# An attention stage whose engine order becomes one planned list, with the first keys and queries placed ahead of the values

## The chip, the core and the metric

The kernel runs on one core of a Trainium2 chip. A core has a matrix engine (TensorE, PE in the profile; its weight loads are shown as PEld), a vector engine (VectorE, DVE), a scalar engine (ScalarE, ACT), a general engine (GpSimd, POOL) and a sync engine (SyncE, SP) that here only issues transfers. Each engine executes its own instructions in the order in which the program wrote them; an instruction whose operand isn't ready holds up all behind it on that engine. Matrix products go to PSUM, eight banks of 128 x 512 numbers; everything else lies in SBUF.

The metric is the device time of one execution in microseconds (us). Three runs of the kernel before took 1886.28, 1887.10 and 1887.19 us, median 1887.1.

## The reference

Two decoder layers work on 512 tokens of width 1024. Layer 0 mixes tokens with a convolution, layer 1 with stick-breaking attention; each has a feed-forward block before and after. Keys and values come from layer 0's output, queries from layer 1:

```python
u = rms_norm(h, mix_norm[layer])
q = split_heads(u @ attn_w_q[i])
o = stick_breaking_attention(q, k_shared, v_shared)
h = h + o @ attn_w_o[i]
```

For each of 16 heads of width 64 the attention computes, with the strict causal mask:

```python
z = q @ k.T * scale
log_remain = reverse_cumsum(log_sigmoid(-z)) - log_sigmoid(-z)
weights = where(causal, exp(log_sigmoid(z) + log_remain), 0)
o = weights @ v
```

## The kernel before

Everything is in 32-bit floats. For precision a matrix product is made of three: each operand is split into a high part (a rounding copy, on ACT) and a low part (the rest, a subtraction on DVE), and `mm3` multiplies high by high, high by low and low by high. Channels lie on the 128 partitions, so a 512 x 1024 matrix is eight tiles of 128 x 512, `res[0]` to `res[7]` for the residual.

The program is a row of stages: feed-forward 0, convolution, feed-forward 1, feed-forward 2, attention, feed-forward 3. The feed-forward blocks (`planned`) and most of the convolution are written as lists: the code adds steps to a `Plan`, each with its engine, an estimated duration, the tiles it reads and writes, and a rank. `Plan.issue` simulates the engines with these durations. Among the steps that could start it takes the one with the earliest start, and of equal ones the one with the lowest rank, and gives its buffers out. Then it emits the steps in the order found, inside a `manual_schedule` block, which keeps that order on PE, DVE, ACT and POOL. SP isn't among these engines. A step marked `port` (the copies on DVE) and every POOL step exclude each other in the simulation. Outside such a block the framework chooses the order by a simulation of its own. In the kernel before, all of attention is left to the framework.

Attention (lines 1273 to 1473) has these parts:

- The residual is sent away to memory (`away`, L1274), because the heads' outputs `ov` take its place; after the last use of a chunk it is brought back (L1461).
- Constants: triangles, the mask and the two matrices `swap`.
- The norm row `rq` (`n_mix.factor`, L1305): token sums on PE (`ss_mix`), an inverse root in a dozen small DVE operations, a diagonal, two matmuls that spread it, a copy on ACT (L389) and a multiplication by the scale on DVE (L1306).
- `project_values(i)` makes the values of two pairs of heads: two weight units and four blocks of 24 matmuls of 256 columns (`pv`), with a copy on ACT and a subtraction on DVE each.
- `project_keys(p)` makes the keys and queries of one pair: 24 matmuls of 512 columns each (`pk`, `pq`), splits, and transfers between partition halves. The queries are multiplied by `rq` behind the product (L1344).
- `head(p, e)` makes one head in three groups of scores (512, 384 and 512 columns). For a group: the scores `z` on PE; Abs, Exp and Ln on ACT (L1390 to L1392); a combination on DVE (L1393); a split in `sh` and `sl` (L1396, L1397, the 384-column subtraction on POOL); triangle sums on PE back into `z` (L1382); Exp on ACT (L1423, `w`); a split in `wh` and `wl` (L1426, L1427); products with the values into `av` (L1433, L1435). At the end of a head a copy `low` (L1439), a matmul with `swap` and a copy into `ov` (L1441). `sh` and `sl` have one buffer for each group; in the last four heads (`DIRECT`) the sums of later groups read those of the earlier ones.
- The output products: `split` of each chunk of `ov` into `oh` and `ol`, then `output` for eight outputs of eight chunks (`po`). For outputs 2 to 5 (`FIRST`) the product over the first six chunks is made ahead and added to the residual, and the last two chunks follow later. Behind each output stand an addition to the residual (L1467) and the next norm's chunk: a scaled copy, its low part, a square and a sum.

PSUM has four banks for `z`, two for `av`, two for `pj` (shared by `pv`, `pk`, `pq` and `po`). Weights come in units of 128 x 1024: three buffers each for the raw unit, its high and its low part; `unit` hands out the one fetched before and fetches the next, and `weight_order` fixes in which order they come.

The order in which the program writes the projections between the heads is a table; entry p + 1 stands behind the heads of pair p, entry 0 ahead of all heads:

```python
PROJECTIONS = (
    (("v", 0), ("kq", 0)), (("kq", 1), ("kq", 2)), (("v", 1),), (("kq", 3), ("kq", 4)), (("v", 2),),
    (("kq", 5), ("kq", 6)), (("v", 3),), (("kq", 7),),
)
```

Of the kernel before, what the change touches and what calls it, by code (L numbers as in the profile page):

```python
# [14 lines left out]
P = 128  # L15
# [24 lines left out]
for _n, _c in _COLS:  # L40
# [34 lines left out]
    (("v", 0), ("kq", 0)), (("kq", 1), ("kq", 2)), (("v", 1),), (("kq", 3), ("kq", 4)), (("v", 2),),  # L75
# [4 lines left out]
FIRST, SIX = (2, 3, 4, 5), 6  # L80
STS = 1
# [27 lines left out]
class Plan:  # L109
# [8 lines left out]
    def __init__(self, room, lag=None):  # L118
        self.room, self.steps, self.last, self.lag = dict(room), [], {}, lag or {}
        self.held, self.kept = {}, ()  # L120
# [19 lines left out]
    def issue(self):  # L140
# [14 lines left out]
        freeing, uses = [], {}  # L155
# [4 lines left out]
        while ready or freeing:  # L160
            best = None
            for n, t in ready.items():
                engine = steps[n][0]
                t = max(t, free.get(engine, 0.0), now)
                if steps[n][6] and port[1] != engine:
                    t = max(t, port[0])
                new = [x for x in steps[n][5] if first[x] == n and x.slot is None]
                if any(len(room[x.kind]) < sum(y.kind == x.kind for y in new) for x in new):
                    continue
                key = (t, steps[n][4])  # L170
                if best is None or key < best[0]:
                    best = (key, n, new)
# [9 lines left out]
            for x in new:  # L182
                x.slot = room[x.kind].pop(0)
# [23 lines left out]
def decoder_kernel(ctx, tc, xin, gu, dna, dnb, pw1, pw2, kq, wv, wo, out):  # L207
# [53 lines left out]
    def weight_order():  # L261
# [25 lines left out]
        for d in range(NC):  # L287
            yield wo[d][:, SIX * P :] if d in FIRST else wo[d]
# [953 lines left out]
    with ExitStack() as c1:  # L1242
# [30 lines left out]
        for c in range(NC):  # L1273
            nc.sync.dma_start(away[:, c * T : (c + 1) * T], res[c])  # L1274
        ov = res
        with ExitStack() as c:
            ap = pool(c, "at")
            ps = pool(c, "psat", space=PSUM)
            ntri = ap.tile([P, P], F32R, name="ntri")
            none = ap.tile([P, P], F32R, name="none")  # L1280
            tri = ap.tile([P, P], F32, name="tri", tag="a", bufs=3)
            G.affine_select(
                out=tri, in_=ones, compare_op=ALU.is_ge, fill=0.0, base=0,
                pattern=[[-1, P]], channel_multiplier=1,
            )
            V.tensor_scalar_mul(ntri, tri, -1.0)

            identb = ap.tile([P, P], BF16, name="identb")
            V.tensor_copy(identb, ident)
            mask = ap.tile([P, T], BF16, name="mask")  # L1290
            V.memset(mask, 0.0)
            V.tensor_scalar_mul(mask[:, :P], tri, MASKED)
            V.tensor_scalar_mul(mask[:, 256:384], ones, MASKED)
            V.tensor_scalar_mul(mask[:, 384:], tri, MASKED)
            V.tensor_scalar_mul(none, ones, -1.0)

            swap = []
            for e in range(2):
                t = ap.tile([P, P], F32R, name=f"swap{e}")
                G.memset(t.bitcast(F32), 0.0)  # L1300
                V.tensor_copy(t[:, HALVES[e][0]], ident[:, HALVES[e][1]])
                swap.append(t)


            rq = n_mix.factor(ps, ("z", "z"), bufs=Z_BANKS)  # L1305
            V.tensor_scalar_mul(rq, rq, HD ** -0.5)  # L1306
            keys, values = {}, {}

            def project_values(i):
                w = [unit() for h in range(2)]  # L1310
                for p in (2 * i, 2 * i + 1):

                    values[p] = ap.tile([P, 4, 4, HD], F32R, name=f"vs{p}", tag="vs", bufs=4)
                for b in range(4):
                    pv = ps.tile([P, T], F32, name=f"pv{i}_{b}", tag="pj", bufs=PJ_BANKS)
                    for k in range(NC):
                        x = at(kvx[k], b * P, P)
                        m = at(w[k // 4], (k % 4) * 256, 256)
                        mm3(pv[:, :256], x, m, k == 0, k == NC - 1)
                    for q in range(2):  # L1320
                        vs = values[2 * i + q]
                        sl = pv[:, q * P : (q + 1) * P].rearrange("p (e d) -> p e d", e=2)
                        A.copy(vs[:, b, 0::3, :], sl)
                        V.tensor_sub(vs[:, b, 1:3, :], sl, vs[:, b, 0::3, :].bitcast(F32))

            def project_keys(p):
                w = unit()
                pk = ps.tile([P, T], F32, name=f"pk{p}", tag="pj", bufs=PJ_BANKS)
                for k in range(NC):
                    mm3(pk, at(w, k * P, P), kvx[k], k == 0, k == NC - 1)  # L1330


                ks = [ap.tile([P, T], F32R, name=f"ks{p}_{e}", tag=f"ks{e}", bufs=3) for e in range(2)]
                kl = tp.tile([P, T], F32R, name=f"kl{p}", tag="sq", bufs=2)
                for e, (own, other) in enumerate(HALVES):
                    A.copy(ks[e][own, :], pk[own, :])
                    V.tensor_sub(kl[own, :], pk[own, :], ks[e][own, :].bitcast(F32))
                    nc.sync.dma_start(ks[e][other, :].bitcast(F32), kl[own, :].bitcast(F32))
                w = unit()
                pq = ps.tile([P, T], F32, name=f"pq{p}", tag="pj", bufs=PJ_BANKS)  # L1340
                for k in range(NC):
                    mm3(pq, at(w, k * P, P), n_mix.x[k], k == 0, k == NC - 1)
                t = tp.tile([P, T], F32, name=f"qt{p}", tag="sq", bufs=2)
                V.tensor_mul(t, pq, rq)  # L1344
                qs = [ap.tile([P, T], F32R, name=f"qs{p}_{e}", tag=f"qs{e}", bufs=3) for e in range(2)]

                ql = [ap.tile([P, T], F32R, name=f"ql{p}_{e}", tag=f"ql{e}", bufs=2) for e in range(2)]
                for e, (own, other) in enumerate(HALVES):
                    A.copy(qs[e][own, :], t[own, :])
                    nc.sync.dma_start(qs[e][other, :].bitcast(F32), qs[e][own, :].bitcast(F32))  # L1350
                    G.memset(ql[e][other, :].bitcast(F32), 0.0)
                    V.tensor_sub(ql[e][own, :], t[own, :], qs[e][own, :].bitcast(F32))
                keys[p] = (ks, qs, ql)

            def head(p, e):


                vs = values[p]
                ks, qs, ql = keys[p]
                h = 2 * p + e  # L1360
                rows = HALVES[e][0]
                z = []
                for g, blocks in enumerate(GROUPS):
                    zt = ps.tile([P, T], F32, name=f"z{h}_{g}", tag="z", bufs=Z_BANKS)
                    n = sum(T - T0[i] for i in blocks)
                    if g == 0:
                        PE.matmul(zt, identb, mask, start=True, stop=False)
                    o = 0
                    for i in blocks:
                        m, blk = T - T0[i], slice(i * P, (i + 1) * P)  # L1370
                        PE.matmul(zt[:, o : o + m], ks[e][:, blk], qs[e][:, T0[i] :],
                                  start=g > 0, stop=False)
                        PE.matmul(zt[:, o : o + m], ks[e][:, blk], ql[e][:, T0[i] :],
                                  start=False, stop=i == 3)
                        o += m
                    if g > 0:
                        PE.matmul(zt[:, :P], identb, mask[:, :P], start=False, stop=True)
                    z.append(zt[:, :n])

                def add(dst, st, pair, a, b):  # L1380
                    for m in pair:
                        PE.matmul(dst, st, m[:, a:b], start=False, stop=True,  # L1382
                                  skip_group_check=True)

                pav = ps.tile([P, T], F32, name=f"av{h}", tag="av", bufs=AV_BANKS)
                later, behind = None, []
                for g, blocks in enumerate(GROUPS):
                    n = z[g].shape[-1]
                    a = ap.tile([P, n], F32, name=f"a{h}_{g}", tag="a", bufs=3)
                    A.activation(a, z[g], AF.Abs)  # L1390
                    A.activation(a, a, AF.Exp, scale=-1.0)
                    A.activation(a, a, AF.Ln, bias=1.0)  # L1392
                    V.scalar_tensor_tensor(a, z[g], 0.0, a, op0=ALU.max, op1=ALU.add)  # L1393
                    sh = ap.tile([P, n], F32R, name=f"sh{h}_{g}", tag=f"sh{g}", bufs=1)
# [275 lines left out]
```

## Time and profile before

| | |
|---|---|
| median of three runs | 1887.1 us |
| profiled execution | 1886.52 us |
| its span, first to last instruction | 1884.8 us |
| mean granted TensorE clock | 0.995 |
| VectorE busy, share of the span | 79% |
| ScalarE busy | 53% |
| GpSimd busy | 12% |
| last matmul of feed-forward 2 starts | 1242.03 us |
| first matmul of feed-forward 3 starts | 1522.78 us |

The profile is of one execution; its times count from the first instruction. A row of the timeline gives start, duration, engine, line, operation, the tile written and the tiles read, and in square brackets how long the engine had been idle and which instruction's end it is thought to have waited for. Matmuls are pipelined: two that start 0.23 us apart each show 0.39 us, so steps between starts tell more than durations. The granted clock is a share of full speed.

### The profile page before, as it was taken

How to read it: one execution, taken by the hardware profiler on the slowest of the kernel's cores; microseconds unless marked ns; L12 is line 12 of the kernel's file. 1: busy time of each engine (PE TensorE's matmuls, PEld its weight loads, DVE VectorE, ACT ScalarE, POOL GpSimd, SP SyncE). 2: the span in 40 equal slices, each digit the busy share in tenths (PEclk: the TensorE clock that was granted, in tenths of full speed). 3: DMA queues.
4: the chain of work that ended last, by engine and by line, in shares of the span. 5: the costliest groups of instructions: out<-in, count | busy, mean ns of one | idle time of the engine just before them, and what ended most of it. 6: DMA issues, size and time to landing. Idle time of an engine off the chain costs nothing.

```text
span 1884.8 us, 29740 instructions
## 1 busy us (share of the span) xinstructions
PE 1859.2 (99%) x11544; PEld 1672.7 (89%) x11544; DVE 1496.3 (79%) x2491; ACT 997.3 (53%) x1673; POOL 221.6 (12%) x243
## 2 busy tenths in 40 slices
PE   9999999999999999999999999999999999999997
PEld 7889989878998999898898999988888779899896
DVE  8968868589889679577985967968999689678595
ACT  5535545696654346255452634647777555345353
POOL 0000000089700000000000000004543100000001
PEclk9999999999999999999999999999999999999998
DMA  5565666644422323323242332452322132323232
GB/s 182 178 218 208 241 217 229 229 168 152 139 68 90 114 89 108 117 87 115 84 163 79 112 112 90 136 160 74 90 84 82 48 112 81 133 71 127 82 110 72
DMA packets 74269, 238.04 MB, mean 126 GB/s; under 512 B 8464, under 2 KB 11152, under 8 KB 74128
## 3 DMA queue, kind: packets, MB, share of 16 engines
q1 hardware_dynamic: 65776, 209.41, 33.7%
q10 hardware_dynamic: 8352, 26.74, 3.6%
q8 instruction: 90, 1.47, 0.3%
q14 instruction: 51, 0.42, 0.1%
HBM read 200.46 MB, written 31.46 MB: 123 GB/s over the span
## 4 chain that ended last, share of the span: by engine, by line
PE 86%; DVE 7%; ACT 2%; DMA 2%; issue 2%; POOL 1%; POOLq 0%; DVEq 0%; ACTq 0%; SPq 0%
PE bank L364 12%; PE bank L365 12%; PE bank L366 12%; PE bank L660 11%; PE bank L661 11%; PE bank L662 11%; PE z L1382 1%; DVE pc L1070 1%; DMA raw<-in_gu_dram 1%; PE pa L365 1%; PE pa L364 1%; PE pa L366 1%; PE po L364 1%; PE po L366 1%; PE po L365 1%
## 5 line engine op out<-in xcount | busy, mean ns | idle before, releaser
L458 ACT CAST high<-raw 128x1024 fp32r<-128x1024 f32 (+1 forms) x199 | 202.5, 1018 | 276.2 <-PE bank L365 220.1
L365 PE MATMUL bank<-hlo,high 128*128 128x512 f32 x686 | 267.1, 389 | 0.0
L364 PE MATMUL bank<-hhi,high 128*128 128x512 f32 x686 | 267.1, 389 | 0.0
L366 PE MATMUL bank<-hhi,low 128*128 128x512 f32 x686 | 266.9, 389 | 0.0
L459 DVE TENSOR_TENSOR low<-raw,high 128x1024 fp32r<-128x1024 f32 (+1 forms) x199 | 234.5, 1178 | 16.3 <-ACT high L458 16.0
L780 DVE SCALAR_TENSOR_TENSOR xpar<-bank,xpar 128x512 f32<-128x512 f32 x93 | 64.3, 691 | 153.7 <-PE bank L366 153.5
L660 PE MATMUL bank<-thi,wh 128*128 128x256 f32 x544 | 154.6, 284 | 1.6 <-ACT u L706 1.2
L660 PE MATMUL bank<-thi,sh 128*128 128x256 f32 x544 | 154.1, 283 | 0.0
L662 PE MATMUL bank<-thi,sl 128*128 128x256 f32 x544 | 154.0, 283 | 0.0
L661 PE MATMUL bank<-tlo,sh 128*128 128x256 f32 x544 | 154.0, 283 | 0.0
L662 PE MATMUL bank<-xhi_f,low 128*128 128x256 f32 x544 | 154.0, 283 | 0.0
L661 PE MATMUL bank<-xlo_f,high 128*128 128x256 f32 x544 | 154.0, 283 | 0.0
L661 PE MATMUL bank<-tlo,wh 128*128 128x256 f32 x544 | 154.0, 283 | 0.0
L662 PE MATMUL bank<-thi,wl 128*128 128x256 f32 x544 | 154.0, 283 | 0.0
L660 PE MATMUL bank<-xhi_f,high 128*128 128x256 f32 x544 | 153.9, 283 | 0.0
L366 PEld LDWEIGHTS bank<-hhi,low 128*128 128x128 f32 x686 | 128.8, 188 | 26.9
L364 PEld LDWEIGHTS bank<-hhi,high 128*128 128x128 f32 x686 | 128.8, 188 | 26.3
L365 PEld LDWEIGHTS bank<-hlo,high 128*128 128x128 f32 x686 | 128.8, 188 | 26.0
L364 PE MATMUL bank<-xhi_f,high 128*128 128x512 f32 x320 | 125.3, 392 | 1.3 <-ACT high L257 1.3
L366 PE MATMUL bank<-xhi_f,low 128*128 128x512 f32 x320 | 124.9, 390 | 0.0
L365 PE MATMUL bank<-xlo_f,high 128*128 128x512 f32 x320 | 124.8, 390 | 0.0
L459 DVE TENSOR_TENSOR sl<-st,sh 128x1024 fp32r<-128x1024 f32 x68 | 83.0, 1221 | 41.1 <-ACT sh L458 41.1
(360 smaller groups left out, 5297.8 us busy)
## 6 DMA issues: line engine op xcount, KB each, us to landing
raw<-in_gu_dram SPq DMA_DIRECT2D x174, 512.0 KB, 3.5
raw<-in_dna_dram SPq DMA_DIRECT2D x64, 512.0 KB, 3.5
plo<-in_pw_dram SPq DMA_DIRECT2D x24, 512.0 KB, 4.2
aparth<-phi ACTq DMA_DIRECT2D x24, 512.0 KB, 3.6
apartl<-plo ACTq DMA_DIRECT2D x24, 512.0 KB, 4.1
raw<-in_dnb_dram SPq DMA_DIRECT2D x32, 384.0 KB, 3.3
high<-aparth SPq DMA_DIRECT2D x21, 512.0 KB, 3.2
low<-apartl SPq DMA_DIRECT2D x21, 512.0 KB, 4.2
```

What stands on the lines that cost most here:

```text
L364: PE.matmul(ps, w[0], x[0], start=first, stop=False)
L365: PE.matmul(ps, w[0], x[1], start=False, stop=False)
L366: PE.matmul(ps, w[1], x[0], start=False, stop=last)
L458: plan.add("A", a, lambda: A.copy(sub(hi()), sub(src())), r=[src], w=[hi], rank=rank)
L459: plan.add("V", v, lambda: V.tensor_sub(sub(lo()), sub(src()), sub(hi()).bitcast(F32)), r=[src, hi], w=[lo], rank=rank)
L660: PE.matmul(d, a[0], b[0], start=start and q == 0, stop=False, skip_group_check=True)
L661: PE.matmul(d, a[0], b[1], start=False, stop=False, skip_group_check=True)
L662: PE.matmul(d, a[1], b[0], start=False, stop=last_, skip_group_check=True)
L780: add("V", 0.62, lambda d=d, pd=pd: V.scalar_tensor_tensor(res[d], pd(), 0.5, res[d], op0=ALU.mult, op1=ALU.add), r=[pd], w=[("res", d)], ...
L1070: add("V", 0.66 * f + 0.06 * half, lambda x=x, q=q: V.scalar_tensor_tensor(pc(), x(), q, pc(), op0=ALU.mult, op1=ALU.add), r=[gl], w=[pc], ...
L1382: PE.matmul(dst, st, m[:, a:b], start=False, stop=True, skip_group_check=True)
```

## The change

Attention becomes a `Plan` too. Its norm row, projections, heads, splits of the outputs, output products and the next norm's chunks are steps of one list, issued in one `manual_schedule` block that follows the list of feed-forward 2. The two heads of pair p have ranks 3p and 3p + 1, the projections behind them 3p + 2 (the first ones -1), the split of an output chunk 3p + 1.5, the norm row -0.95, the way out of the residual -0.9, and the outputs 24 and up. The plan gets a rule for some buffers (`fifo`): they are given out in the order of ranks, and round in a ring. The first keys and queries stand ahead of the first values, also in the order of weights. Queries 0 go to an `av` bank instead of a `pj` bank. The scale of `rq` is applied in its copy on ACT. The outputs with all chunks and those with two left alternate (`LAST`). The constants and the number of buffers stay.

```diff
 PROJECTIONS = (
-    (("v", 0), ("kq", 0)), (("kq", 1), ("kq", 2)), (("v", 1),), (("kq", 3), ("kq", 4)), (("v", 2),),
+    (("kq", 0), ("v", 0)), (("kq", 1), ("kq", 2)), (("v", 1),), (("kq", 3), ("kq", 4)), (("v", 2),),
...
+LAST = (2, 0, 3, 1, 4, 6, 5, 7)
...
+        for n in sorted(range(len(steps)), key=lambda n: steps[n][4]):
+            for x in steps[n][5]:
+                if x.kind in self.fifo and first[x] == n and x.slot is None:
+                    turn.setdefault(x.kind, []).append(x)
...
+                if any(x.kind in turn and (turn[x.kind][0] not in new or (taken.get(x.kind, -1) + 1) % self.room[x.kind] not in room[x.kind]) for x in new):
+                    continue
...
-        for d in range(NC):
+        for d in LAST:
             yield wo[d][:, SIX * P :] if d in FIRST else wo[d]
...
+                plan = Plan(room, lag=LAG)
+                plan.fifo = ("z", "av", "pj", "vs", "sq", "ks0", "ks1", "qs0", "qs1", "ql0", "ql1", "sh0", "sl0", "sh1", "sl1", "sh2", "sl2")
...
+                add("V", HEAD[0], lambda: None, rank=-9)
+                add("joint", HEAD[1], lambda: None, w=["acc_in"], rank=-9)
+                ss, pb = tile("z"), tile("z")
+                add("PE", 0.5, lambda: token_sums(ss()[:, :4], n_mix.acc), r=["acc_in"], w=[ss], rank=-0.95)
...
+                add("V", 2.9, root, r=[ss], w=["root"], rank=-0.95)
...
+                add("A", 0.6, lambda: A.activation(rq, pb(), AF.Copy, scale=HD ** -0.5), r=[pb], w=["rq"], rank=-0.95)
+                add("A", 1.3, lambda: A.preload_act_table_set("natural_log_exp_and_others"), w=["exp"], rank=-1.5)
...
+                for k in range(NC):
+                    add("D", 0.9, lambda k=k: nc.sync.dma_start(away[:, k * T : (k + 1) * T], res[k]), w=[("ov", k)], rank=-0.9)
...
+                    pq = tile("pj" if p else "av")
...
+                        add("V", 0.27 * f + 0.07, lambda a=a, sh=sh: V.tensor_copy(sh(), a()), r=[a], w=[sh], rank=rank, port=True)
+                        eng, cost = (("G", 1.25 * f), ("V", 0.53 * f + 0.07))[g not in SL_POOL]
+                        add(eng, cost, lambda a=a, sh=sh, sl=sl, eng=eng: (G if eng == "G" else V).tensor_sub(sl(), a(), sh().bitcast(F32)),
+                            r=[a, sh], w=[sl], rank=rank)
...
+                for p in range(-1, NC):
+                    if p >= 0:
+                        head(p, 0, 3 * p)
+                        head(p, 1, 3 * p + 1)
+                    for what, i in PROJECTIONS[p + 1] if p < NC - 1 else ():
+                        (project_values if what == "v" else project_keys)(i, 3 * p + 2)
...
+                rank = 3 * NC
+                for d in FIRST:
+                    output(d, 0, SIX, rank)
+                    rank += 1
+                for d in LAST:
+                    output(d, SIX if d in FIRST else 0, NC, rank)
+                    chunk(d, rank + 0.2)
+                    rank += 1
```

Here `f` is a group's share of 512 columns, "A", "V", "G" and "D" are ACT, DVE, POOL and the transfers, and the number behind the engine is the estimated duration in us.

More of the change, by code (lines that the diff above doesn't have):

```diff
@@ L119, in __init__ @@
         self.room, self.steps, self.last, self.lag = dict(room), [], {}, lag or {}
-        self.held, self.kept = {}, ()
+        self.held, self.kept, self.fifo = {}, (), ()
     def add(self, engine, work, do, r=(), w=(), rank=0, port=False):
@@ L182, in issue @@
             for x in new:
-                x.slot = room[x.kind].pop(0)
+                i = room[x.kind][0]
+                if x.kind in turn:
+                    turn[x.kind].remove(x)
+                    taken[x.kind] = taken.get(x.kind, -1) + 1
+                    i = taken[x.kind] % self.room[x.kind]
+                room[x.kind].remove(i)
+                x.slot = i
             ends[n] = t + work
@@ L1272, in decoder_kernel @@
         away = spill.tile([P, NC * T], F32, name="away")
[L1273 to L1274 removed]
+        n_f2 = Norm("f2_1", "ffn2_1")
         ov = res
[L1276 to L1315, printed above, removed]
[L1316 to L1445 removed]
@@ L1446, in decoder_kernel @@
                 for p in range(-1, NC):
                     if p >= 0:
-                        head(p, 0)
-                        head(p, 1)
+                        head(p, 0, 3 * p)
+                        head(p, 1, 3 * p + 1)
                     for what, i in PROJECTIONS[p + 1] if p < NC - 1 else ():
-                        (project_values if what == "v" else project_keys)(i)
-            n_f2 = Norm("f2_1", "ffn2_1")
-            ox = []
-            for p in range(NC):
-                hi = kvp.tile([P, T], F32R, name=f"oh{p}", tag="hi", bufs=NC)
-                lo = kvp.tile([P, T], F32R, name=f"ol{p}", tag="lo", bufs=NC)
-                split(hi, lo, ov[p])
-                ox.append((hi, lo))
-                nc.sync.dma_start(res[p], away[:, p * T : (p + 1) * T])
@@ L1462, in output @@
-            def output(d, a, b, more):
-                w = unit()
-                pp = ps.tile([P, T], F32, name=f"po{d}_{a}", tag="pj", bufs=PJ_BANKS)
-                for k in range(a, b):
-                    mm3(pp, at(w, (k - a) * P, P), ox[k], k == a, k == b - 1)
-                V.tensor_add(res[d], pp, res[d])
-                if not more:
-                    n_f2.chunk(d)
-            for d in FIRST:
-                output(d, 0, SIX, True)
-            for d in range(NC):
-                output(d, SIX if d in FIRST else 0, NC, False)
+                        (project_values if what == "v" else project_keys)(i, 3 * p + 2)
@@ new lines, in attention @@
+                ox = []
+                for p in range(NC):
+                    hi, lo = (Buf("-", lambda p=p, n=n: kvp.tile([P, T], F32R, name=f"o{n[0]}{p}", tag=n, bufs=NC)) for n in ("hi", "lo"))
+                    rank = 3 * p + 1.5
+                    add("A", 0.55, lambda p=p, hi=hi: A.copy(hi(), ov[p]), r=[("ov", p)], w=["kvx", hi], rank=rank)
+                    add("V", 0.6, lambda p=p, hi=hi, lo=lo: V.tensor_sub(lo(), ov[p], hi().bitcast(F32)), r=[("ov", p), hi], w=["kvx", lo], rank=rank)
+                    add("D", 0.9, lambda p=p: nc.sync.dma_start(res[p], away[:, p * T : (p + 1) * T]), w=[("ov", p), ("res", p)], rank=rank)
+                    add(("back", p), 1.5, lambda: None, w=[("res", p)], rank=rank)
+                    ox.append((hi, lo))
@@ new lines, in square @@
+                def square(nrm, d, rank):
+                    if nrm.n == 0:
+                        add("A", 0.55, lambda: A.activation(nrm.acc, res[d], AF.Square), r=[("res", d)], w=["acc"], rank=rank)
+                    else:
+                        sq = tile("sq", dtype=F32)
+                        add("A", 0.55, lambda: A.activation(sq(), res[d], AF.Square), r=[("res", d)], w=[sq], rank=rank)
+                        add("V", 0.6, lambda: V.tensor_add(nrm.acc, nrm.acc, sq()), r=[sq], w=["acc"], rank=rank)
+                    nrm.n += 1
@@ new lines, in output, with chunk, lower @@
+                def output(d, a, b, rank):
+                    w = unit(rank)
+                    pp = tile("pj")
+                    for k in range(a, b):
+                        pe(pp, lambda k=k, w=w: at([x() for x in w], (k - a) * P, P), lambda k=k: [x() for x in ox[k]],
+                           [*w, *ox[k]], rank, k == a, k == b - 1)
+                    add("V", 0.6, lambda: V.tensor_add(res[d], pp(), res[d]), r=[pp], w=[("res", d)], rank=rank)
+                def chunk(d, rank):
+                    n_f2.order.append(d)
+                    g = col(n_f2.gain, d)
+                    hi, lo = (Buf("-", lambda d=d, n=n: xp.tile([P, T], F32R, name=f"x{n}_f2_1_{d}", tag=f"x{n}", bufs=NC)) for n in ("hi", "lo"))
+                    add("A", 0.65, lambda: A.activation(hi(), res[d], AF.Copy, scale=g), r=[("res", d)], w=[hi], rank=rank)
+                    def lower():
+                        V.scalar_tensor_tensor(lo(), res[d], g, hi().bitcast(F32), op0=ALU.mult, op1=ALU.subtract)
+                        n_f2.x[d] = (hi(), lo())
+                    add("V", 0.66, lower, r=[("res", d), hi], w=[lo], rank=rank)
+                    square(n_f2, d, rank)
@@ new lines, in attention @@
+                rank = 3 * NC
[6 more added lines that the diff above has]
+                    rank += 1
+                while len(held) < 1:
+                    fetch_unit(rank)
+                plan.kept = [x for w in held for x in w]
+                with tc.manual_schedule(engines={nc.tensor.engine, nc.vector.engine, nc.scalar.engine, nc.gpsimd.engine}):
+                    plan.issue()
@@ L1476, in decoder_kernel @@
+                ready.extend((hi(), lo(), hi.slot, lo.slot) for hi, lo in held)
+                for j, x in enumerate((high_turn, low_turn)):
+                    slots = [w[2 + j] for w in ready]
+                    x.sort(key=lambda i: (i in slots, slots.index(i) if i in slots else 0))
+        attention()
     n_out = Norm("out", None)
```

271 lines of the change are left out of this document (224 added, 47 removed).

## The prediction

> **What bounds the kernel now.** I read the page's head first, then busy time by stretches, then PE's waits between 1228 and 1540 us, then the timeline where the waits lie.
>
> ```profile
> span 1884.8 us, 29740 instructions
> PE 1859.2 (99%) x11544; PEld 1672.7 (89%) x11544; DVE 1496.3 (79%) x2491; ACT 997.3 (53%) x1673; POOL 221.6 (12%) x243
> ```
> ```profile
> 640.00:930.00 290.00, 290.00 (x1839) 264.47 (x1838) 220.64 (x353) 130.67 (x199) 0.00 (x0) 1.00 0.30 100
> ...
> 1242.30:1275.00 32.70, 31.82 (x190) 28.32 (x190) 19.50 (x54) 12.57 (x22) 0.00 (x0) 1.00 0.37 115
> 1275.00:1447.60 172.60, 171.32 (x985) 146.45 (x984) 160.69 (x262) 128.31 (x246) 82.32 (x84) 1.00 0.28 82
> 1447.60:1496.00 48.40, 48.40 (x255) 40.85 (x253) 38.71 (x65) 32.40 (x60) 8.47 (x8) 1.00 0.20 63
> 1496.00:1506.10 10.10, 7.43 (x18) 4.54 (x17) 3.88 (x6) 4.50 (x9) 0.00 (x0) 0.68 0.10 28
> 1506.10:1512.60 6.50, 5.72 (x23) 3.84 (x22) 6.32 (x10) 5.75 (x10) 0.00 (x0) 0.98 0.25 82
> ```
>
> Columns: stretch, its length, busy us of PE, PEld, DVE, ACT, POOL, then the granted clock. TensorE is the bound nearly everywhere; the feed-forward stage of the first row has no idle time at all. Attention runs from 1242.3 to 1522.8. No matmul goes away in this change, so all that it can win is what PE loses in these 280 us: idle time, and time at a low clock.
>
> ```profile
> PE po L364 <- ACT oh L257: 1.3, 1, 1.3
> PE pv L364 <- ACT high L257: 0.9, 1, 0.9
> PE av L1440 <- ACT low L1439: 0.7, 1, 0.7
> PE av L1435 <- DVE wl L1427: 0.6, 2, 0.3
> ```
>
> The waits are few and small. The largest cluster is at the end:
>
> ```profile
> 1495.95 0.33 PE L1435 MATMUL av<-wl,vs 128*128 128x384 f32 x1
> 1496.62 0.50 PE L1433 MATMUL av<-wh,vs 128*128 128x512 f32 x1 [0.33 <-DVE wh L1426]
> 1497.41 0.49 PE L1435 MATMUL av<-wl,vs 128*128 128x512 f32 x1 [0.29 <-DVE wl L1427]
> 1498.63 0.50 PE L1440 MATMUL av<-low,swap 128*128 128x512 f32 x1 [0.73 <-ACT low L1439]
> 1500.46 1.22 PE L364 MATMUL po<-oh,high 128*128 128x512 f32 x2 [1.32 <-ACT oh L257]
> ...
> 1505.62 0.63 PE L366 MATMUL po<-oh,low 128*128 128x512 f32 x1
> 1506.05 0.56 PE L364 MATMUL po<-oh,high 128*128 128x512 f32 x1
> 1506.44 0.39 PE L365 MATMUL po<-ol,high 128*128 128x512 f32 x1
> 1506.67 0.40 PE L366 MATMUL po<-oh,low 128*128 128x512 f32 x1
> ```
> ```profile
> 1447.60:1496.00 48.40, 31.16 (x114) 20.77 (x114) 2.66 (x4) 1.00 0.20 63
> 1496.00:1522.80 26.80, 21.57 (x78) 16.05 (x78) 4.81 (x7) 0.87 0.28 89
> ```
>
> The last fence counts the output products (tile po): 114 start before 1496, 78 after. From 1495.95 PE has nothing left but the last head, and follows its chain (wh, wl, low, oh) until 1500.46: 4.5 us for 4 matmuls. The step between matmuls is 0.23 us (1506.44 to 1506.67), so 4.5 - 0.9 = **3.6 us** idle. Then the 13 matmuls up to 1506.44 go at 0.43 us instead of 0.23 (1505.62 to 1506.05), in the stretch whose granted clock is 0.68: 6.0 - 3.0 = **3.0 us**. From 1506.1 to 1512.6 the 23 matmuls would need 5.3 of the 6.5 us, and DVE is busy 6.32 of them: **1.2 us**, lost to late evacuations. The middle (1275 to 1447.6) loses 172.6 - 171.3 = **1.3 us**. The start:
>
> ```profile
> 1242.03 0.39 PE L366 MATMUL bank<-hhi,low 128*128 128x512 f32 x1
> 1243.29 0.36 PE L364 MATMUL pv<-high,kvh 128*128 128x256 f32 x1 [0.88 <-ACT high L257]
> ```
> ```profile
> 1242.45 0.69 DVE L780 SCALAR_TENSOR_TENSOR xpar<-bank,xpar 128x512 f32<-128x512 f32 x1 [0.73 <-PE bank L366]
> ```
>
> 1.26 between two starts instead of 0.23: **1.0 us**. The profile names a weight cast, but by the code the two units of the values were fetched before that one; I read the wait as one for pv's bank, which the last evacuation of the feed-forward (L780) leaves at 1243.14. In all 3.6 + 3.0 + 1.2 + 1.3 + 1.0 = 10.1 us, half a per cent: about the most that this change can win.
>
> **The change part by part.** The same engine instructions are issued but for one: the row's scaling (a DVE multiply) goes into ACT's copy. 192 output matmuls, the projections, the heads and 8 DMAs out and back stay. What moves:
>
> *Start.* Keys and queries 0 (48 matmuls) come first. Their first tile has another bank than pv had, and its weights are the unit already held. The order of the list alone doesn't fix the bank, so the saving lies between 0 and 1.0; I take **-1.0**. The second unit's cast now stands in the list behind an activation-table load on ACT, but 24 matmuls (5.5 us) of keys hide both, on ACT and DVE alike. The 8 away transfers go through SP, whose order the list doesn't hold; their rank only orders them in the plan. No head writes over their source before about 40 us later, so I cost them nothing; if a weight load lands behind them, the price is a late unit as at the start, about 1 us.
>
> *Heads begin earlier.* Rows:
>
> ```profile
> 1249.12 0.95 PE L396 MATMUL ss_mix<-onesD,acc_mix 128*128 128x1 f32 x8
> ...
> 1257.08 0.59 ACT L389 COPY r_mix<-pb_mix 128x512 f32<-128x512 f32 x1
> ```
> ```profile
> L1371 PE MATMUL z<-qs,ks x64: 277/338/477, 1275.1 to 1485.1; 128*128 128x256 f32 x32, 128*128 128x384 f32 x16, 128*128 128x512 f32 x16
> ```
>
> The norm row takes 8.6 us from its sums to its copy. Before, the order was values, keys and queries 0, then 1, and the first score at 1275.1. Now the row can form under queries 0 and the values, and the first score follows these: 48 x 0.23 = 11.0, sums 1.0, and the values' 96 matmuls of half width 11.6 (two of their four blocks, 48 matmuls, filled 1243.29 to 1249.12, 0.121 each), together 23.6 after 1242.3, that is 1265.9: 9.2 us earlier. How much of this reaches the last head isn't in the trace: PE was 99% busy in the middle, and a head that runs sooner pushes a projection later. Heads have the lower rank, so they go first where both are ready. Bounds 0 and 9.2; I take **6**.
>
> *The last head's order.* Its first low part was ready at 1483.94, but PE took its half of the sum at 1487.43:
>
> ```profile
> 1482.62 1.32 DVE L1397 TENSOR_TENSOR sl<-a,sh 128x512 fp32r<-128x512 f32 x1
> ```
> ```profile
> 1486.13 0.39 PE L1382 MATMUL z<-sh,ntri 128*128 128x512 f32 x1
> ...
> 1487.43 0.39 PE L1382 MATMUL z<-sl,ntri 128*128 128x512 f32 x1
> ```
>
> A list that takes head steps ahead of outputs when both are ready can gain between 0 and 3.5 us here; I take **2**.
>
> *Less to hide behind.* The outputs can only run ahead of the last head with chunks 0 to 6. Before: 4 first parts x 18 matmuls and, with two banks, two whole products' 21 each: 72 + 42 = 114, the very count of the row. Now the third and fourth bank users are outputs 2 (its rest: 3 matmuls ahead of chunk 7) and 0 (21): 72 + 24 = 96. So PE runs dry 18 x 0.23 = 4.1 us sooner, and 96 matmuls remain behind the last head instead of 78. This is the change's cost.
>
> *Sum at the end.* PE runs dry at 1495.95 - 1.0 - 4.1 = 1490.85. The last head's output is ready at 1500.46 - 6 - 2 = 1492.5. Between lie the same 4 matmuls, 0.9 us, so PE idles 0.75 instead of 3.6: -2.85. The clock stayed 1.00 in the stretch with the 0.88 us idle, so I let it stay here: -3.0. The order 2, 0, 3, 1, 4, 6, 5, 7 puts a product of 24 matmuls (5.5 us) behind each of 6 (1.4 us), so that DVE's three operations per output no longer end the wait: 0.3 left of 1.2, -0.9.
>
> By the Trainium skill, "TensorE: Matmul & The Clock Gate", section "What's actually happening", the clock halves after an idle window of about 3.4 us. The trace agrees: 3.6 us of idle in 4.5 and then half speed. By that rule too 0.75 us would keep the clock.
>
> *The middle.* The new list can remove the 1.3 us or add waits; the upper price is the rival below. I take **+1.0**.
>
> Total: -1.0 - 2.85 - 3.0 - 0.9 + 1.0 = -6.75. The profiled execution took 1886.52 us (span 1884.8 and 1.7 around it): 1879.8. The median of the three runs is 1887.1, 0.6 above the profiled one, so in their measure **1880.3**.
>
> **The rivals.**
>
> *The early start doesn't arrive (same).* PE paces the middle, the heads end where they did but for the start's 1.0 and 2.0 of order: 1497.5. Then 96 matmuls take 22.1, the clock is lost again (the idle is 5.7): 1497.5 + 22.1 + 3.0 + 0.3 = 1522.9 against 1522.8, so 1886.6, or 1887 as median. For it: PE at 99% from 1275 to 1447.6. Against it: ranks.
>
> *The row comes no sooner than before (same).* Its rank is -0.95, behind the values' -1; if PE has no gap when the sums are ready, they go after the values, and the first score stays near 1275. The change then doesn't bring the heads forward at all. With 3.5 us from the last head's order, the output is ready at 1500.5 - 1.0 - 3.5 = 1496.0, and it ends at 1496 + 22.4 = 1518.4, or 1521.4 with the clock lost: 1882 to 1885, middle 1883.8, as median 1884.4.
>
> *The list trusts durations that DVE doesn't keep (slower).* PE executes in the order written; a late operand stops all behind it, outputs that could have run among them. The list gives a 512-wide low part (sl) 0.60 us on DVE and holds only copies, not subtractions, apart from POOL:
>
> ```profile
> L1397 DVE TENSOR_TENSOR sl<-a,sh 128x512 fp32r<-128x512 f32 x32 | 33.4, 1045 | 1.3
> ...
> L1337 DVE TENSOR_TENSOR kl<-pk,ks 64x512 fp32r<-64x512 f32 x16 | 10.9, 684 | 2.1 <-ACT ks L1336 1.9
> ```
>
> The same width without a second SBUF input (kl reads PSUM) takes 684 ns, sl 1045: (1.045 - 0.684) x 32 = 11.6 us that the list doesn't know. If half falls where PE has nothing ready, 5.8 us, and the heads arrive late as in the first rival: 1886.6 + 5.8 = 1892.4, about 1893 as median; all of it would give 1898. It decides for slower when the waits behind sl and wl pass 4 us without the end's gain. Against it: the same collisions exist now, and PE waits only 1.3 us in the middle.
>
> The Trainium skill, "SBUF — State Buffer", section "Who interferes with whom", says that a Vector instruction with two SBUF inputs contends with a GpSimd instruction that reads SBUF, and the later fully blocks. The trace agrees with it (sl 1045 ns against 684). It speaks against the list, which marks only the copies.
>
> **How the numbers follow.** Forecast (gains arrive in part or in full) 0.56; the start doesn't arrive 0.13; the row no sooner 0.12; DVE late 0.19. A measurement of this kernel can tell about 0.2%, 3.8 us, from no change: faster below 1883.3, slower above 1890.9. So faster 0.56, same 0.25, slower 0.19. The range begins where all 10.1 us are won and a little more of the small restarts goes, 1875.5, and ends just above the slower rival's half price, 1894.
>
> **What would show it.** Right: keys' first matmul within 0.4 us of 1242.3; first score near 1266; idle at the last head under 1.5 us and clock 1.00 in every stretch after; 96 output matmuls behind the last head's result; attention about 273 us long. Wrong: first score near 1275; PE waits on sl or wl (DVE or POOL) summing above 4 us between 1275 and 1450; half-clock steps of 0.43 us among the outputs again.

## The result, and the profile after

The change made the kernel slower: 2009.35 us (six runs, 2007.78 to 2011.42) against 1886.57 us before on the same chip (six runs, 1884.54 to 1887.19). The ratio is 1.0654, interval 1.0643 to 1.0666. The forecast was 1880.3.

The head of the page of the kernel after, its slices of granted clock, and the chain that ended last:

```profile
span 2006.7 us, 29799 instructions
PE 1902.9 (95%) x11542; PEld 1699.1 (85%) x11544; DVE 1480.6 (74%) x2490; ACT 1118.8 (56%) x1765; POOL 219.0 (11%) x243
...
PEclk9999999999999999999999999978898999999999
...
PE 80%; ACT 11%; issue 3%; DVE 3%; DMA 2%; POOL 1%; POOLq 0%; ACTq 0%; DVEq 0%; SPq 0%
```

PE has the same matmuls as before. ACT has 92 instructions more (1765 against 1673) and 121.5 us more busy time (1118.8 against 997.3). The slow slices are those of attention. Busy time of attention in the kernel before and then in the kernel after (columns as in the prediction):

```profile
1242.30:1522.80 280.50, 274.90 (x1508) 232.42 (x1508) 237.28 (x406) 188.00 (x350) 90.79 (x92) 0.99 0.27 83
```
```profile
1244.20:1644.60 400.40, 317.38 (x1506) 257.26 (x1507) 222.17 (x408) 308.96 (x442) 88.24 (x92) 0.89 0.20 59
```

Attention is 119.9 us longer, which is nearly all of the span's 121.9. ACT is busy 121.0 us more in it. PE shows 42.5 us more, at a clock of 0.89, and 83.0 us idle instead of 5.6. What ACT does there, grouped by line (the engine, the operation, its count, busy us, mean ns, idle before):

```profile
L1503 ACT ACT_TABLE_LOAD x45 | 57.7, 1283 | 0.8
...
L1502 ACT ACT_TABLE_LOAD x24 | 30.8, 1283 | 0.4
...
L1538 ACT ACT_TABLE_LOAD x22 | 28.2, 1283 | 1.1 <-PE z L1466 0.7
```

These are the lines of the heads' Ln (L1503), first Exp (L1502) and second Exp (L1538): 91 loads of activation tables, 116.7 us. The kernel before has none at these lines. Two stretches of the timeline of the kernel after, ACT first:

```profile
1280.49 1.28 ACT L1502 ACT_TABLE_LOAD   x1
1281.78 1.04 ACT L1502 ACTIVATE a<-a 128x512 f32<-128x512 f32 x2
1282.85 1.28 ACT L1503 ACT_TABLE_LOAD   x1
1284.14 1.04 ACT L1503 ACTIVATE a<-a 128x512 f32<-128x512 f32 x2
```
```profile
1289.53 0.40 PE L379 MATMUL pj<-kvh,low 128*128 128x512 f32 x1
1291.98 0.39 PE L1466 MATMUL z<-sh,none 128*128 128x256 f32 x1 [2.05 <-DVE sh L1533]
1293.60 0.45 PE L1466 MATMUL z<-qs,ks 128*128 128x384 f32 x1 [1.24 <-ACT w L1538]
```

Each time Exp and Ln alternate, a table is loaded; steps of the same function in a row share one load. PE then waits for ACT, or for DVE steps that wait for ACT. PE's largest waits now (what waits, for what, us in total, times, the longest):

```profile
PE z L1466 <- ACT w L1538: 34.2, 12, 6.5
PE av L1466 <- ACT w L1556: 18.3, 7, 4.9
PE av L1466 <- DVE wh L1540: 12.8, 10, 4.0
PE z L1466 <- DVE sh L1507: 7.9, 8, 1.9
```

Why are they loaded? The list does hold the load of the set that has both functions (`natural_log_exp_and_others`). Where it ran, by its line in the kernel before (L1444) and in the kernel after (L1402), and below that the Silu line of the feed-forward in the kernel after (count, duration, first and last start):

```profile
L1444 ACT ACT_TABLE_LOAD  x1: 1283/1283/1283, 1210.1 to 1210.1; - x1
```
```profile
L1402 ACT ACT_TABLE_LOAD  x1: 1283/1283/1283, 6.2 to 6.2; - x1
```
```profile
L687 ACT ACT_TABLE_LOAD  x2: 1283/1283/1283, 36.9 to 1658.7; - x2
```

In the kernel after it ran at 6.2 us, 1238 us ahead of attention, and at 36.9 Silu loaded its own table again. Attention then began with Silu's table, and each change between Exp and Ln loaded another one. In the kernel before, L1443 (`tc.issue_after(last[0].ins)`) held the load behind the last Silu of feed-forward 2. The change drops this line. The load has no operand and is ACT's first step in the list, so nothing of the list stands ahead of it on ACT.

The start of attention is as forecast: between the last feed-forward product and the first one of the keys lie 0.23 us.

```profile
1244.17 0.39 PE L379 MATMUL bank<-hhi,low 128*128 128x512 f32 x1
1244.40 0.39 PE L377 MATMUL pj<-kvh,high 128*128 128x512 f32 x1
```

At its end there is a small new wait of 0.88 us. The kernel before has no idle time at that place (1522.78); all planned lists below have this wait.

```profile
1644.61 0.47 PE L377 MATMUL bank<-xhi_f,high 128*128 128x512 f32 x1 [0.88 <-ACT high L471]
```

### The profile page after: what moved, and what is told of

Its sections match the earlier page's. It is cut to its first block, busy times and chain, and to the rows that moved or that the text cites. A ratio compares the mean times of both kernels' runs of the same rounds, so it can differ in the third digit from the quotient of the medians.

```text
span 2006.7 us, 29799 instructions
## 1 busy us (share of the span) xinstructions
PE 1902.9 (95%) x11542; PEld 1699.1 (85%) x11544; DVE 1480.6 (74%) x2490; ACT 1118.8 (56%) x1765; POOL 219.0 (11%) x243
## 4 chain that ended last, share of the span: by engine, by line
PE 80%; ACT 11%; issue 3%; DVE 3%; DMA 2%; POOL 1%; POOLq 0%; ACTq 0%; DVEq 0%; SPq 0%
PE bank L377 11%; PE bank L378 11%; PE bank L379 11%; PE bank L673 10%; PE bank L675 10%; PE bank L674 10%; PE pj L377 2%; ACT L1503 2%; PE pj L378 2%; PE pj L379 2%; ACT L1502 2%; PE z L1466 1%; DMA raw<-in_gu_dram 1%; ACT L1538 1%; ACT a L1502 1%
## 5 line engine op out<-in xcount | busy, mean ns | idle before, releaser
L471 ACT CAST high<-raw 128x1024 fp32r<-128x1024 f32 (+1 forms) x235 | 236.6, 1007 | 289.5 <-PE bank L378 219.3
L472 DVE TENSOR_TENSOR low<-raw,high 128x1024 fp32r<-128x1024 f32 (+1 forms) x235 | 276.7, 1178 | 28.6 <-ACT high L471 28.2
```

The lines of the kernel that those rows point to most:

```text
L471: plan.add("A", a, lambda: A.copy(sub(hi()), sub(src())), r=[src], w=[hi], rank=rank)
L472: plan.add("V", v, lambda: V.tensor_sub(sub(lo()), sub(src()), sub(hi()).bitcast(F32)), r=[src, hi], w=[lo], rank=rank)
```

## The experiments

The theory: the early load is the whole loss, and the list itself is about as fast as forecast. The rival: the list itself is slow, and the loads hide beside PE's work.

**The load held in its place** (fix).

```diff
-add("A", 1.3, lambda: A.preload_act_table_set("natural_log_exp_and_others"), w=["exp"], rank=-1.5)
+def table():
+    with tc.issue_after(last[0].ins):
+        A.preload_act_table_set("natural_log_exp_and_others")
+add("A", 1.3, table, w=["exp"], rank=-1.5)
```

> The changed kernel with one edit: the load of the table that holds both Exp and Ln is queued behind the last Silu of feed-forward 2, as in the kernel before, instead of standing free as the first step of the list. Theory (table loads): the 91 loads of 1.283 us at Exp and Ln inside attention and the second Silu load near 37 us go; ACT busy falls from 1119 to about 1000 us, and the time from 2009 to 1876-1890, about the time first forecast (1880). Rival (late DVE operands, tight list): the loads go but PE still waits on sh, sl, wh, wl for tens of us, time above 1895. If the list itself is worth nothing: 1885-1890.

Measured: 1894.83 us (1893.92 to 1897.25) against 1885.54, ratio 1.0050 (1.0037 to 1.0062). The load runs at 1211.2, and no other line of attention has one:

```profile
L1405 ACT ACT_TABLE_LOAD  x1: 1283/1283/1283, 1211.2 to 1211.2; - x1
```

So holding the load saves 2009.35 - 1894.83 = 114.5 us, 1.26 us for each of the 91 loads that go; attention alone is 400.4 - 289.4 = 111.0 us shorter. What is left, 9.3 us against before, is the list's own. The time lies between the two expectations: the loads are nearly the whole loss, but the list isn't as fast as forecast.

**The same fault alone, in the kernel before** (before_float): the load isn't held, and neither is attention held behind it.

```diff
-with tc.issue_after(last[0].ins):
-    table = A.preload_act_table_set("natural_log_exp_and_others")
-with tc.issue_after(table.ins):
+A.preload_act_table_set("natural_log_exp_and_others")
+if True:
```

> The kernel before with one edit: the table load is no longer queued behind the last Silu. Theory (table loads): it moves to the start of the program, Silu loads its own table again, and about 94 more loads appear in attention. ACT is busy some 190 of the 280 us of attention; 94 x 1.283 = 121 us more make at least 310, so the time rises by at least 30 us, and by up to 120 if the loads lie on the chain of the heads as in the changed kernel: 1917-2010. Rival (the planned order is what costs): the framework's order hides the loads, within 10 us of 1887.

Measured: 1965.81 us (1963.26 to 1967.69), ratio 1.0422 (1.0408 to 1.0437), 80.3 us more. The load ran at 6.0 us, and the heads' lines have 93:

```profile
L1392 ACT ACT_TABLE_LOAD x46 | 59.0, 1283 | 0.8
L1423 ACT ACT_TABLE_LOAD x31 | 39.8, 1283 | 1.5 <-DVE wl L1427 1.0
L1391 ACT ACT_TABLE_LOAD x16 | 20.5, 1283 | 0.3
```

The lost place alone makes the loads, without any list. There it costs 0.86 us of the end time for each load, in the change's list 1.26. The 0.86 also holds whatever else changed in an order that is no longer queued behind the load.

**The load behind another step of the list** (second): in the plan its step reads the sums of the norm row (`ss`), so it isn't ACT's first step any more. The instruction itself still has no operand, and there is no `issue_after`.

```diff
-add("A", 1.3, lambda: A.preload_act_table_set("natural_log_exp_and_others"), w=["exp"], rank=-1.5)
+add("A", 1.3, lambda: A.preload_act_table_set("natural_log_exp_and_others"), r=[ss], w=["exp"], rank=-0.95)
```

> The changed kernel with one edit: the table load isn't the first ACT step of the list any more (it reads the token sums' tile and has the row's rank), and is still not queued behind the last Silu. Theory (only the first step of a list floats, since an order is kept only between its steps): the load stays inside attention, no loads at Exp and Ln, time within 4 us of the mended kernel's 1895. Rival (the load floats wherever it stands in the list unless queued): some 90 loads and about 2009 us.

Measured: 1895.59 us (one run). The load runs inside attention, at 1249.7, still 26 us ahead of the first score (1275.7):

```profile
L1402 ACT ACT_TABLE_LOAD  x1: 1283/1283/1283, 1249.7 to 1249.7; - x1
```

On ACT, copies of the keys (from 1248.50) stand ahead of it. So the list's order does hold a load that has a step of the list ahead of it; as the first step it floated.

All kernels that follow hold the load as fix does; their diffs are against fix. The table splits attention at the last head's last matmul (`swap`). "Front" is the time from the start of attention to there, less 0.2265 us (the step of an output matmul) for each output matmul already made; "tail" is the time from there to the end, less 0.2265 for each that remained. Both come from the starts of PE's rows, attention being 1242.03 to 1522.78 in the kernel before.

| kernel | median us | attention | first score after | outputs ahead / behind | front | tail |
|---|---|---|---|---|---|---|
| before | 1885.35 to 1886.3 | 280.8 | 33.1 | 114 / 78 | 230.8 | 6.5 |
| fix | 1894.83 | 289.4 | 33.1 | 81 / 111 | 243.5 | 2.4 |
| fix_vfirst | 1899.27 | 292.2 | 34.1 | 81 / 111 | 246.3 | 2.3 |
| fix_last | 1900.82 | 294.9 | 33.1 | 69 / 123 | 248.3 | 3.0 |
| fix_dve | 1893.77 | 288.2 | 33.1 | 93 / 99 | 241.6 | 3.1 |
| fix_port | 1909.04 | 301.9 | 33.1 | 78 / 114 | 256.7 | 1.7 |
| fix_slack | 1894.65 | 288.5 | 24.5 | 93 / 99 | 241.9 | 3.1 |
| dur_slack | 1894.07 | 289.0 | 24.5 | 96 / 96 | 241.5 | 3.9 |
| excl_slack | 1888.15 | 283.6 | 24.5 | 87 / 105 | 238.3 | 1.7 |
| fix_port_slack | 1883.08 | 276.5 | 24.5 | 96 / 96 | 229.2 | 3.8 |
| more_slack | 1894.40 | 287.5 | 35.2 | 96 / 96 | 240.1 | 3.9 |

In fix the tail is 4.1 us shorter than before and the front 12.7 longer.

**Values first again** (fix_vfirst).

```diff
-    (("kq", 0), ("v", 0)), (("kq", 1), ("kq", 2)), (("v", 1),), (("kq", 3), ("kq", 4)), (("v", 2),),
+    (("v", 0), ("kq", 0)), (("kq", 1), ("kq", 2)), (("v", 1),), (("kq", 3), ("kq", 4)), (("v", 2),),
```

> The mended kernel with the values first again, also in the order of weights. If the forecast's step holds (keys first let the heads start about 9 us sooner, 6 of it arriving): 3-6 us slower than the mended kernel, first score about 9 us later. If PE paces the middle, or the row stays behind the values: within 1.5 us of it.

Measured: 1899.27 us (1896.10 to 1899.66), ratio 1.0067 (1.0055 to 1.0080). Keys first is worth some 4 us in this list, but only 1.0 of it is at the first score, where 9 were expected. So the gain comes from another place than the forecast's step.

**Outputs in plain order** (fix_last).

```diff
-LAST = (2, 0, 3, 1, 4, 6, 5, 7)
+LAST = (0, 1, 2, 3, 4, 5, 6, 7)
```

> The mended kernel with the eight outputs in the order 0 to 7 instead of 2, 0, 3, 1, 4, 6, 5, 7. Forecast's step: 18 more output matmuls can run ahead of the last head (114 instead of 96), worth up to 4.1 us if PE would wait there, against about 0.9-1.2 us for late evacuations behind it. If PE idles at the last head: 1-4 us faster than the mended kernel; if the last head's result comes in time anyway: 0.5-1.5 us slower.

Measured: 1900.82 us (1899.89 to 1901.46), ratio 1.0079 (1.0065 to 1.0093). The alternating order is worth 6.0 us in this list. Plain order was to bring 18 output matmuls more ahead of the last head; it brought 12 fewer (69 against 81). PE has one gap of 3.3 us in front of an output product, before the last heads are done:

```profile
1475.37 0.47 PE L377 MATMUL pj<-oh,high 128*128 128x512 f32 x1 [3.33 <-DVE sq L1445]
```

The front of fix is next. First its stretch from 1275 to 1447.6, in which PE was busy for 171.32 of 172.60 us in the kernel before, then PE's waits over all of attention:

```profile
1275.00:1447.60 172.60, 166.29 (x925) 135.64 (x924) 145.81 (x246) 118.47 (x230) 80.19 (x82) 1.00 0.23 68
```
```profile
PE av L1471 <- DVE wh L1545: 2.4, 6, 0.6
PE av L1471 <- DVE wl L1547: 1.2, 5, 0.3
PE z L1471 <- DVE sl L1514: 1.0, 4, 0.3
...
PE z L1471 <- POOL sl L1539: 0.4, 2, 0.2
```

6.3 us idle instead of 1.3, and 60 matmuls fewer. Not all that the front loses shows as idle time, since a matmul's row lasts 0.39 us where the step is 0.23, and a short wait hides in it. By the steps between starts, less the usual step of the same width, I estimate that PE loses some 21 us ahead of matmuls into z and av in the front of fix, and some 10 in the kernel before. The difference is nearly all of the 12.7. One such wait, seen on DVE, POOL and PE:

```profile
1299.37 1.10 DVE L1545 CAST wh<-w 128x512 fp32r<-128x512 f32 x1
```
```profile
1299.18 1.01 POOL L1514 TENSOR_TENSOR sl<-a,sh 128x384 fp32r<-128x384 f32 x1
```
```profile
1300.53 0.39 PE L1471 MATMUL av<-wh,vs 128*128 128x256 f32 x1 [0.58 <-DVE wh L1545]
```

The copy took 1.10 us, the mean of its group is 0.614, and a subtraction of POOL ran beside it. The list does hold copies and POOL apart in its simulation, so here its times had slipped; DVE's subtractions it doesn't hold apart at all, as the prediction's third rival said. The theory from this: late steps of DVE that collide with POOL make the front long. One thing speaks against it: taken over their groups of 512 columns, DVE's steps in fix aren't slower than before. `sl` takes 801 ns (1045 before), `wl` 787 (775), `wh` 614 (556), `sh` 563 (506). The next four kernels test the theory.

**No subtractions on POOL** (fix_dve).

```diff
-SL_POOL = (1,)
-WL_POOL = (1,)
+SL_POOL = ()
+WL_POOL = ()
```

> The mended kernel with the 32 subtractions of 384 columns (sl and wl of the middle group) on DVE instead of POOL. If collisions are the cause: fewer waits of PE on sl, wh and wl, 2-8 us faster, although DVE gets 32 x 0.55 = 18 us more work. If DVE's own load is the cause (it is busy over 90% of the middle): 3-15 us slower.

Measured: 1893.77 us (1892.91 to 1894.23), ratio 1.0042 (1.0029 to 1.0055): 1 us less than fix, which isn't clear of noise, and neither of the two expectations.

**The list knows of the collisions** (fix_port): DVE's subtractions with two SBUF inputs (`low`, `ql`, `sl`, `wl`, `ol`) exclude POOL's steps in the simulation, and POOL's durations are those of the trace.

```diff
-eng, cost = (("G", 1.25 * f), ("V", 0.53 * f + 0.07))[g not in SL_POOL]
+eng, cost = (("G", 1.12 * f + 0.18), ("V", 0.53 * f + 0.07))[g not in SL_POOL]
...
-    r=[a, sh], w=[sl], rank=rank)
+    r=[a, sh], w=[sl], rank=rank, port=True)
```

> The mended kernel with other durations in the attention's list alone: the DVE subtractions with both inputs in SBUF (low, sl, wl, ql, ol) exclude POOL in the list's simulation as the copies do, and POOL's steps get the durations that the trace shows (0.53 to 1.3 us). No instruction is added or taken away. Theory (operands late because DVE and POOL collide outside the list's knowledge): the middle of attention, which loses about 23 us against 6 in the kernel before, loses under 14, and the time falls by 6-14 us, to 1881-1889. Rival (the list is tight in general, its lags too short): change within 3 us.

Measured: 1909.04 us (1907.86 to 1911.68), ratio 1.0125 (1.0110 to 1.0141), 14 us more than fix. DVE's `sl` fell to a mean of 721 ns (801 in fix), so its collisions became fewer or shorter (`wl` stayed, 796 against 787). PE waited more all the same, for POOL and for a DVE that comes late:

```profile
PE av L1471 <- POOL wl L1547: 4.9, 5, 2.3
PE z L1471 <- DVE sh L1512: 3.0, 4, 1.3
```

**Longer lags** (fix_slack): in the simulation of attention a result on DVE, ACT or POOL counts as late by more than before.

```diff
-plan = Plan(room, lag=LAG)
+plan = Plan(room, lag={**LAG, "V": 0.8, "A": 0.5, "G": 0.6})
```

> The mended kernel with longer lags between engines in the attention's list alone (behind DVE 0.8 us instead of 0.2, behind ACT 0.5 instead of 0.2, behind POOL 0.6 instead of 0.15), so that PE is given other matmuls for longer before it takes a head's. Theory (a tight order, whatever makes operands late): the losses of the middle fall to under 12 us and the time by 6-14 us, to 1881-1889, although DVE and POOL collide as before. Rival (collisions are what slows the heads, slack only shifts it): within 3 us, or slower because the last head comes later.

Measured: 1894.65 us (1893.68 to 1897.40), ratio 1.0051 (1.0039 to 1.0064), the same as fix. The norm row's copy now comes 15.6 us after the start of attention (24.2 in fix), and the first score 8.6 us sooner, but the front is only 1.6 us shorter.

**Both together** (fix_port_slack).

> Both edits, the exclusions with measured POOL durations and the longer lags. If they mend the same loss: as the better of the two within 2 us. If they mend different losses: 3-6 us faster than the better one, 1877-1884, which would be faster than the kernel before.

Measured: 1883.08 us (11 runs, 1881.32 to 1884.55) against 1885.35 (15 runs), ratio 0.9985 (0.9976 to 0.9994). It is the only version that beats the kernel before, by 2.3 us. The front is 229.2, and the last head's chain ends in one wait:

```profile
1495.06 0.39 PE L1471 MATMUL av<-w,swap 128*128 128x512 f32 x1
1496.77 0.50 PE L377 MATMUL pj<-oh,high 128*128 128x512 f32 x1 [1.32 <-ACT oh L1576]
```

**Its two parts, each with the longer lags**: the exclusions alone (excl_slack), POOL's durations alone (dur_slack).

> Longer lags with the exclusions of subtractions and POOL alone, POOL's durations as in the change. If the exclusions are what the longer lags need: within 3 us of both together (1883). If the durations are: about 1895, as the lags alone.

> Longer lags with POOL's measured durations alone, without the exclusions. If the durations are what the longer lags need: within 3 us of 1883. If the exclusions are: about 1895, as the lags alone.

Measured: 1888.15 us (1886.74 to 1890.72), ratio 1.0011 (1.0002 to 1.0020), and 1894.07 us (1893.18 to 1895.32), ratio 1.0040 (1.0027 to 1.0054). By the ratios, beside the lags alone (1.0051) the exclusions save 0.40% or 7.5 us, the durations 0.11% or 2.1 (not clear of noise), and both 0.66% or 12.4. So the exclusions bring the larger part, but alone they don't come within 3 us of both, as was expected if they were the cause.

**Still longer lags** (more_slack): fix_port_slack with 1.1, 0.6 and 1.0.

> Exclusions, measured durations and still longer lags (1.1 us behind DVE, 0.6 behind ACT, 1.0 behind POOL). The middle loses about 9 us with 0.8, 0.5 and 0.6, against 6 in the kernel before. If waits of late operands are still what it loses: 1-3 us faster, 1880-1882. If the longer lags only push the last head later: 1-5 us slower.

Measured: 1894.40 us (1894.15 to 1895.77), ratio 1.0043 (1.0030 to 1.0057). The first score is late again, at 35.2, and by the ratios 0.58% or 10.9 us are lost against fix_port_slack: more lag isn't better in itself.

## Why the prediction was wrong

The step that failed is in "Start": "The second unit's cast now stands in the list behind an activation-table load on ACT, but 24 matmuls (5.5 us) of keys hide both". I costed the load at nothing, as an instruction that stays where the list puts it. I counted what the change adds and moves, but not the edge that it takes away (L1443). The load left its place, 91 others came, and with the load held again 114.5 us of the 122.8 go (fix); without the list, the same lost edge costs 80.3 (before_float). Both are shown. That the cover of 24 matmuls would hide one load in its place is right: in second it runs inside attention at 1249.7, and the time is that of fix.

The Trainium skill, "ScalarE: Activation LUTs", section "Table sets: the hidden batching unit", says that Ln and then Exp take one table load, as `natural_log_exp_and_others` has both. The runs agree only where that set is the active one: 1 load for attention in fix, 91 in the kernel after. By its section "What ACT_TABLE_LOAD costs", a switch takes about 1283 ns for the load and about 1380 ns for a drain. The load agrees; of the drain the trace shows nothing (a load from 1280.49 to 1281.77, the next activation at 1281.78).

The other steps, read from kernels that hold the load:

- Start, -1.0: right. The two products stand 0.23 us apart instead of 1.26.
- Heads earlier, first score 23.6 us behind the start: wrong in the change's list. It came after 33.1, as before, and by the second rival's mechanism: the two matmuls that spread the row stand behind all 96 matmuls of the values, so its copy comes 24.2 us after the start (1267.34 below), later than in the kernel before (15.1). With longer lags it came after 24.5, near the forecast. Even then the time wasn't there at the last head: the front of fix_slack is 11.1 us longer than before, and only in fix_port_slack is it shorter, by 1.6. So "I take 6", for a carry of the 9.2, wasn't borne out by the list as written. In fix_port_slack the last head's last matmul stands 5.7 us sooner than before (250.9 against 256.6; 6 + 2 = 8 was forecast); 18 output matmuls fewer ahead of it are 4.1 us of this, the rest is the front's 1.6, of which 1.0 is the gain at the start.

```profile
1267.34 0.60 ACT L1401 ACTIVATE r_mix<-z 128x512 f32<-128x512 f32 x1
```

- Outputs: 96 ahead and 96 behind was forecast. fix has 81 and 111 (the cause stays open); fix_port_slack has 96 and 96.
- Idle at the last head 0.75 and the clock kept: nearly right. fix has no idle time there, fix_port_slack 1.32 and a little behind it, and both keep 1.00:

```profile
1505.00:1532.00 27.00, 25.84 (x113) 20.76 (x111) 19.28 (x28) 15.57 (x24) 0.00 (x0) 1.00 0.41 131
```
```profile
1495.00:1518.50 23.50, 21.85 (x94) 17.14 (x94) 18.98 (x27) 14.83 (x23) 0.00 (x0) 1.00 0.39 129
```

- The tail as a whole fell from 6.5 to 2.4 (fix) or 3.8 (fix_port_slack). So the gains forecast for the end (2.85 + 3.0 + 0.9) are real in good part; some of the idle time among them lies ahead of the split and so in the front.
- The alternating order of the outputs, -0.9: right in sign; it is worth 6.0 in fix, most of it ahead of the last head, where I had not looked.
- The last head's order, -2: right. Its first low part waited 3.5 us for PE before, 0.95 in fix (ready at 1493.01, taken at 1493.96) and 1.6 in fix_port_slack, a gain of 2.5 and 1.9:

```profile
1492.33 0.68 DVE L1514 TENSOR_TENSOR sl<-a,sh 128x512 fp32r<-128x512 f32 x1
```
```profile
1493.96 0.39 PE L1471 MATMUL z<-sl,ntri 128*128 128x512 f32 x1
```

- Middle, +1.0: the sign is right, the size wrong. fix's front is 12.7 us longer than before, although the start and the last head's order gained. The third rival had priced half of DVE's lateness at 5.8 and all of it at 11.6; its 1893 to 1898 is where fix lies.
- Two sums of the rivals are off by a little: the middle of the second rival's 1882 to 1885 is 1883.6, not 1883.8, and 1886.6 + 11.6 is 1898.8 as a median, not 1898. Neither changes the forecast.

For the list alone, then, the third rival was nearest in time, in good part by luck. Its price isn't there: `sl` took 801 ns, so that the term is (0.801 - 0.684) x 32 = 3.7 us instead of 11.6, and PE's idle time behind sl and wl adds up to 2.6 us (1.2 + 1.0 + 0.4), under the 4 that the rival had named. DVE's copies and subtractions do run beside POOL's, and PE does wait for them. But taking POOL's `sl` and `wl` of the middle group away gave 1 us, and telling the list of the collisions, with POOL's measured durations, cost 14. Only the collisions and longer lags together, with POOL's measured durations, won the front back. What makes the list's front 12.7 us long is therefore not shown. Why each alone doesn't, and why fix_port is so slow, stays open: each of these settings makes another order of the whole list, and the runs compare such orders, not single waits. For the same reason the 4 and 6 us of fix_vfirst and fix_last are no prices of one step.

## What to carry to other kernels

When a diff moves a step into another ordering regime, list the ordering edges that it removes, and ask of each instruction without operands, such as a table load, what still holds it there; in this kernel nothing held the first step of the list. Price such an instruction by what follows if it runs somewhere else, not by its duration in its place. A list written from estimated durations may need its collisions and its slack right together; test such settings in pairs as well as one by one.

## What the runs showed of the hardware

- A change of table took its 1283 ns on ACT and no more that the trace shows: the next activation starts 0.01 us behind the load. With ACT feeding PE in a chain, most of that time reached the end: 1.26 us per load in the change's list (what the lower clock cost is in it), 0.86 in the order of before_float.
- PE's granted clock fell to 0.89 over attention in the kernel after, and its busy time rose by 42.5 us. The end moved by 119.9 us, about what ACT gained in busy time (121.0); I take from this, without a run of its own, that the low clock lay inside waits for ACT and cost little more.
- A copy on DVE of 128 x 512 took 1.10 us beside a POOL subtraction (fix), against a mean of 0.614 for its group.
